# Differential attention's queries and keys: two token-major products of 256 columns made into one of 512

## The chip, the core and the metric

The kernel runs on one core of a Trainium2 chip. The metric is the device time of one execution in microseconds (us); lower is better. The time before is the median of three runs, and one more execution was profiled.

## What is computed

Two layers of a hybrid trunk run over 384 tokens of width 1024: 128 context tokens and 256 latent tokens, which share all weights. A layer normalises its input, then runs three token mixers in parallel (a convolution module, differential attention, latent attention), merges them with gates, and ends in an MLP. The part that matters here is the projection of the normalised input `h` to the queries, keys and values of differential attention: three matrices of 1024 by 512, four heads of 2 times 64 columns each. Queries and keys are normalised over each 64 columns, and for the latent tokens rotated:

```python
proj = h @ P['w_in'][l]
u_conv, dq, dk, dv, cq, ckv, kpe, gl = jnp.split(proj, _split_points(), axis=-1)
q = _rms(dq.reshape(b, s, DIFF_HEADS, 2, DIFF_HD), P['diff_q_norm'][l])
k = _rms(dk.reshape(b, s, DIFF_HEADS, 2, DIFF_HD), P['diff_k_norm'][l])
v = dv.reshape(b, s, DIFF_HEADS, 2 * DIFF_HD)
...
q = _rope2d(q, tabs[0])
k = _rope2d(k, tabs[0])
```

The normalised keys and the values of the context tokens are outputs too.

## The kernel before

**Weights.** All weights lie in DRAM as pieces (`weight_pieces`, L69) of at most 1024 elements per partition, in the order in which they are used. A piece is loaded by SP (`raw`, L179), then split (`split`, L191) into a high part by ScalarE (L197) and a remainder by VectorE (L198). Four buffers hold high parts, three hold remainders. Every product takes three matmuls per block of 128 rows of the contraction (`passes`, L204 to L206): high by high, high by remainder, remainder by high.

**Two forms of product.** In the feature-major form (`fm`) the weights are stationary in the array and 384 token columns stream through. In the token-major form (`tm`, L229) a block of 128 tokens of `h` is stationary and columns of the weights stream through, 256 at a time for queries, keys and values. The projection has 8 blocks of contraction, 3 blocks of tokens and 3 passes, so one token-major product is 72 matmuls, whatever its columns. Each block of tokens accumulates in a PSUM bank of its own; the three `mm` banks are shared by all such products.

**The part that is changed.** `qkv(l, h, c)` (L594) runs twice per layer, once for each pair of heads c. It makes three products in a row: queries, keys, values (with 32 more columns for c = 1). After the products of queries and keys, ScalarE copies each bank to a tile `tok` (L619) and squares it (L591), VectorE sums the squares (L592), takes the reciprocal root in ten short operations (L309 to L319) and rotates (L581 to L585); the keys are scaled first (L634, L636). Then a flag `q0`, `k0`, `v0` and so on is raised.

**What orders the work.** Three generators are woven together (`weave`, L253): the dense products, the chain of transposes (`chains`), and the two attentions. A dense step tells how much of a unit it is worth (a unit is three passes of 384 columns, so three passes of 256 columns are 2/3). A side generator waits for a flag, then for a number of units from the table `W` (L134), then issues its next step. `qkv_T` (L642) waits for `q0`, then 12.5 units, and transposes the queries (L658); it then waits for `k0`, then 20 units, and transposes the keys. Attention c starts on the flags `kT` and `v` of that c. Where the dense generator itself waits for a flag, `weave` issues side steps without regard to their units until the flag is up. Such a place is `mla_kv` (L884): before the second half of its products it yields `mqT0` or `mqT1` (L893), which `mla_T` raises; for the second group of heads `mla_T` first waits for `m0` (L924), which the latent attention raises after its first pair of heads. After the weave a scheduler orders the instructions of each engine: it goes by priority, which follows the order of issue, and takes later work where the earlier isn't ready. So the convolution's long row of VectorE operations (L1071), which is issued late, fills VectorE's free time much earlier.

Of the kernel before, what the change touches and what calls it, by code (L numbers as in the profile page):

```python
# [17 lines left out]
ALU = mybir.AluOpType  # L18
# [3 lines left out]
P = 128  # L22
D = 1024
KD = 8
# [4 lines left out]
NT = 3  # L29
# [11 lines left out]
EPS = 1e-6  # L41
# [27 lines left out]
def weight_pieces():  # L69

    out = []

    def add(key, name, l, nkb, cols, per):
        for i, k0 in enumerate(range(0, nkb, per)):
            out.append(((l, *key, i), name, l, range(k0, min(k0 + per, nkb)), cols))

    def r(a, n):
        return list(range(a, a + n))

    def mod(l, s):  # L80
        for p in range(MODS[s][3]):
            a = MODS[s][0] * D + MODS[s][1] * p * P
            add(("mod", s, p), "mod_w", l, KD, r(a, P) + r(a + MODS[s][2] * P, P), 4)

    mod(0, 0)
    for l in range(L):
        for i in range(1 if l == 0 else AB):
            add(("u", i), "w_in", l, KD, r(512 + P * i, P) + r(P * i, P), 4)
        for c in range(2):
            for i in range(3):  # L90

                e = r(3200, 32) if (i, c) == (2, 1) else []
                add(("qkv", i, c), "w_in", l, KD, r(1024 + 512 * i + 256 * c, 256) + e, 3 if e else 4)
        add(("c", 0), "w_in", l, KD, r(2560, 256), 4)
        add(("c", 1), "w_in", l, KD, r(2816, 256), 4)
        add(("c", 2), "w_in", l, KD, r(3072, P), 8)
        for i in range(1 if l == 0 else AB, 4):
            add(("u", i), "w_in", l, KD, r(512 + P * i, P) + r(P * i, P), 4)
        for g in range(2):
            add(("uq", g), "w_uq", l, 3, r(384 * g, 384), 2)  # L100
            add(("ukv", g), "w_ukv", l, 2, r(512 * g, 512), 2)
            for i in range(4):
                add(("g", 1 + g, i), "w_in", l, KD, r(3232 + 1024 * (1 + g) + 256 * i, 256), 4)
            for i in range(4):
                n, w = (("od", "w_diff_out"), ("om", "w_mla_out"))[g]
                add((n, i), w, l, 4, r(256 * i, 256), 4)
        if l == 0:
            mod(0, 2)
            mod(0, 1)
        for i in range(4):  # L110
            add(("g", 0, i), "w_in", l, KD, r(3232 + 256 * i, 256), 4)
            add(("oc", i), "w_conv_out", l, 4, r(256 * i, 256), 4)
        for i in range(4):
            add(("wo", i), "w_out", l, KD, r(256 * i, 256), 4)
        for f in range(2):
            for i in range(8):
                add(("up", f, i), "w_up", l, KD, r(2048 * f + 256 * i, 256), 4)
            for i in range(4):
                for j, k0 in enumerate(range(16 * f, 16 * f + 16, 4)):
                    out.append(((l, "dn", f, i, j), "w_down", l, range(k0, k0 + 4), r(256 * i, 256)))  # L120
    return out


PIECES = weight_pieces()
WOFF = {}
_o = 0
# [20 lines left out]
class Body:  # L147
# [446 lines left out]
    def qkv(self, l, h, c):  # L594

        V, A, t = self.V, self.A, self.t
        d = self.d[c]
        v = self.tl(self.ap, [P, 4, 256], "v", 3)
        cs = slice(256 * c, 256 * c + 256)
        self.nc.gpsimd.dma_start(out=v[:, 3, :], in_=t["cv"][l][:, cs])  # L600
        d["v"] = v
        for i in range(3):
            if i < 2:
                xs = self.tl(self.ap, [P, NT, 256], "tok", 2)
                ss = self.tl(self.ap, [P, NT * 4], "ss", 2)
            pss = [self.psum("mm") for _ in range(NT)]
            e = (i, c) == (2, 1)
            yield from self.tm(pss, 288 if e else 256, [(l, "qkv", i, c, k) for k in range(3 if e else 2)],
                               [self.tok(h, tt) for tt in range(NT)])
            if e:  # L610
                self.pe = self.tl(self.ap, [P, 4, 32], "pe", 1)
                self.nc.sync.dma_start(out=self.pe[:, 3, :], in_=t["cpe"][l])
            for tt, ps in enumerate(pss):
                if i == 2:
                    A.copy(v[:, tt, :], ps[:, :256])
                    if e:
                        V.tensor_copy(self.pe[:, tt, :], ps[:, 256:288])
                    continue
                A.copy(xs[:, tt, :], ps[:, :256])  # L619
                self.sumsq(ss[:, 4 * tt : 4 * tt + 4], xs[:, tt, :].rearrange("p (n d) -> p n d", d=64), 0.125, 4, 64)  # L620
            if i == 2:
                self.nc.scalar.dma_start(out=t["nv"][l][:, cs], in_=v[:, 0, :])
                self.flags.add(f"v{c}")
                continue
            V.tensor_scalar(ss, ss, EPS, None, op0=ALU.add)
            y = self.rsqrt(ss, NT * 4)
            x4 = xs.rearrange("p t (n d) -> p t n d", d=64)
            if i == 0:
                d["qsc"] = self.tl(self.ap, [P, 32], "qsc", 3)[:, : NT * 4]
                V.tensor_scalar(d["qsc"], y, 0.125, None, op0=ALU.mult)  # L630
                self.rope(x4[:, 1:3], self.tab["dq"], 4, 64)
            else:
                xf = xs.rearrange("p t (n d) -> p (t n) d", d=64)
                V.tensor_tensor(xf, xf, y.unsqueeze(2).to_broadcast([P, NT * 4, 64]), ALU.mult)  # L634
                dk = self.rowt[:, ROW["dk"][0] : ROW["dk"][1]]
                V.tensor_tensor(x4[:, 0], x4[:, 0], dk.unsqueeze(1).to_broadcast([P, 4, 64]), ALU.mult)  # L636
                self.nc.scalar.dma_start(out=t["nk"][l][:, cs], in_=xs[:, 0, :])
                self.rope(x4[:, 1:3], self.tab["dk"], 4, 64)
            d["qk"[i]] = xs
            self.flags.add(f"{'qk'[i]}{c}")  # L640

    def qkv_T(self, l, c):  # L642

        A, E = self.A, self.E
        d = self.d[c]
        for i in range(2):
            yield f"{'qk'[i]}{c}"
            yield W["qT"] if i == 0 else W["kT"]
            if i == 0:
                dst = d["qT"] = self.tl(self.ap, [P, 2, T], "qT", 3)  # L650
            else:
                dst = d["kT"] = self.tl(self.ap, [P, 2, NK], "kT", 3)
                self.nc.gpsimd.dma_start(out=dst[:, :, T:], in_=self.t["ckT"][l][:, 2 * c : 2 * c + 2, :])
            xs = d["qk"[i]]
            for hh in range(2):
                pt = self.psum("tr")
                for j in range(NT):
                    E.transpose(pt[:, j * P : j * P + P], xs[:, j, hh * P : hh * P + P], self.ident)  # L658
                if i == 0:
                    a, b = PV["dq"]  # L660
                    A.activation(dst[:, hh, 0:P], pt[:, 0:P], AF.Identity, scale=self.pv[l][:, a:b])
                    A.copy(dst[:, hh, P:T], pt[:, P:T])
                else:
                    A.copy(dst[:, hh, 0:T], pt[:, :T])
        self.flags.add(f"kT{c}")
# [827 lines left out]
```

## Time and profile before

| what | us |
|---|---|
| median of three runs | 1348.26 |
| lowest and highest run | 1346.23, 1349.81 |
| the profiled execution | 1349.73 |
| its span in the trace | 1347.9 |
| TensorE busy | 1325.7 (98%) |
| TensorE weight loads | 1252.0 (93%) |
| VectorE busy | 1058.2 (79%) |
| ScalarE busy | 681.3 (51%) |

The profiled execution lies 1.47 us above the median, and its span 1.83 us below its own time. A busy TensorE isn't a TensorE at its peak: a matmul's recorded duration includes its latency and overlaps the next, so its cost in a stream is read from the distance between two starts.

### The profile page before, as it was taken

The numbers are of one execution on the slowest core, as the hardware profiler recorded it, in microseconds if no ns is written. First come the engines' busy times: TensorE is split into PE (matmuls) and PEld (weight loads), VectorE is DVE, ScalarE is ACT, GpSimd is POOL, SyncE is SP. The second block draws the span as 40 slices with busy tenths as digits, with TensorE's granted clock in tenths as the row PEclk, the third lists the DMA queues.
The fourth block names the chain that finished last, engine by engine and source line by source line (L and its number), as shares of the span: only waits on it lengthen the run. The fifth ranks groups of instructions, "written<-read, shape, count | busy, mean of one in ns | idle before, by whom it ended". The sixth has DMA issues, their size and how long they took to land.

```text
span 1347.9 us, 21768 instructions
## 1 busy us (share of the span) xinstructions
PE 1325.7 (98%) x8096; PEld 1252.0 (93%) x8096; DVE 1058.2 (79%) x2517; ACT 681.3 (51%) x1281; POOL 16.7 (1%) x34
## 2 busy tenths in 40 slices
PE   5999999999999999999999999999999999999998
PEld 3999887879999999999999998888899999999998
DVE  5877999995998999974569779999999899333432
ACT  3555655454544762365335556665554467226621
POOL 0000000000000000000000000000000000000000
PEclk8999999999999999999999999999999999999999
DMA  9533334456574477764444333222347445333341
GB/s 361 187 96 113 123 127 148 156 175 216 162 254 131 145 245 248 253 203 126 149 149 141 99 97 114 69 95 94 125 163 244 157 157 188 125 126 126 127 148 54
DMA packets 62683, 209.46 MB, mean 155 GB/s; under 512 B 7840, under 2 KB 13600, under 8 KB 62320
## 3 DMA queue, kind: packets, MB, share of 16 engines
q1 hardware_dynamic: 56304, 196.93, 44.8%
q0 software_dynamic: 1808, 6.63, 1.5%
q10 hardware_dynamic: 4464, 4.50, 0.9%
q8 instruction: 64, 1.05, 0.3%
q14 instruction: 43, 0.35, 0.1%
HBM read 203.54 MB, written 4.49 MB: 154 GB/s over the span
## 4 chain that ended last, share of the span: by engine, by line
PE 93%; DVE 4%; DMA 1%; SPq 1%; ACT 0%; issue 0%; DVEq 0%
PE mm L204 19%; PE mm L206 19%; PE mm L205 19%; PE sc L204 9%; PE sc L205 9%; PE sc L206 9%; PE sc L759 3%; DMA wr<-wts 1%; PE av L996 1%; PE tr L981 1%; DVE wl L198 1%; PE mm L367 1%; PE av L821 1%; DVE z L1071 1%; PE tr L945 1%; PE tr L774 1%
## 5 line engine op out<-in xcount | busy, mean ns | idle before, releaser
L197 ACT CAST wh<-wr 128x1024 fp32r<-128x1024 f32 (+3 forms) x280 | 290.0, 1037 | 371.2 <-PE mm L205 189.5
L198 DVE TENSOR_TENSOR wl<-wr,wh 128x1024 fp32r<-128x1024 f32 (+3 forms) x280 | 336.7, 1203 | 132.6 <-PE mm L206 66.1
L204 PE MATMUL mm<-h,wh 128*128 128x384 f32 x848 | 291.2, 343 | 0.0
L206 PE MATMUL mm<-h,wl 128*128 128x384 f32 x848 | 286.3, 338 | 0.2 <-DVE wl L198 0.2
L205 PE MATMUL mm<-h,wh 128*128 128x384 f32 x592 | 200.1, 338 | 0.5 <-DVE h L440 0.5
L204 PEld LDWEIGHTS mm<-h,wh 128*128 128x128 f32 x848 | 159.8, 188 | 7.0 <-issue 2.9
L206 PEld LDWEIGHTS mm<-h,wl 128*128 128x128 f32 x848 | 159.5, 188 | 1.6 <-DVE wl L198 0.8
L1071 DVE SCALAR_TENSOR_TENSOR z<-u,dwh,z 128x399 f32<-128x399 f32 x240 | 147.2, 629 | 0.4
L395 DVE SCALAR_TENSOR_TENSOR ot<-wm,srow 128x1024 bf16<-128x1024 f32 x112 | 136.7, 1220 | 2.8 <-DMA wm<-modwT 2.2
L205 PEld LDWEIGHTS mm<-h,wh 128*128 128x128 f32 x592 | 111.6, 189 | 1.7 <-DVE h L440 0.8
L206 PE MATMUL sc<-h,wl 128*128 128x384 f32 x336 | 112.6, 335 | 0.0
L204 PE MATMUL sc<-h,wh 128*128 128x384 f32 x336 | 112.6, 335 | 0.0
L205 PE MATMUL mm<-o,wh 128*128 128x384 f32 x320 | 107.4, 336 | 0.0
L204 PE MATMUL mm<-x,wh 128*128 128x384 f32 (+1 forms) x288 | 97.3, 338 | 0.0
L206 PE MATMUL mm<-x,wl 128*128 128x384 f32 (+1 forms) x288 | 96.6, 336 | 0.0
L205 PE MATMUL mm<-x,wh 128*128 128x384 f32 (+1 forms) x288 | 96.6, 335 | 0.0
L204 PE MATMUL sc<-x,wh 128*128 128x384 f32 (+1 forms) x272 | 91.7, 337 | 0.0
L205 PE MATMUL sc<-x,wh 128*128 128x384 f32 (+1 forms) x272 | 91.2, 335 | 0.0
L206 PE MATMUL sc<-x,wl 128*128 128x384 f32 (+1 forms) x272 | 91.2, 335 | 0.0
L204 PE MATMUL mm<-wh,h 128*128 128x256 f32 (+1 forms) x288 | 83.1, 289 | 0.0
L206 PE MATMUL mm<-wh,h 128*128 128x256 f32 (+1 forms) x288 | 82.1, 286 | 0.0
L205 PE MATMUL mm<-wl,h 128*128 128x256 f32 (+1 forms) x288 | 82.0, 285 | 0.0
(275 smaller groups left out, 2564.7 us busy)
## 6 DMA issues: line engine op xcount, KB each, us to landing
wr<-wts SPq DMA_DIRECT2D x306, 512.0 KB, 3.5
wm<-modwT SPq DMA_DIRECT2D x56, 512.0 KB, 4.3
srow<-condrow POOLq DMA_DIRECT2D x2, 1024.0 KB, 7.7
wr<-wts SPq DMA_DIRECT2D x4, 432.0 KB, 3.4
G<-xT SPq DMA_DIRECT2D x8, 192.0 KB, 4.1
wr<-wts SPq DMA_DIRECT2D x4, 384.0 KB, 3.1
G<-xT POOLq DMA_DIRECT2D x8, 192.0 KB, 3.4
xd<-G ACTq DMA_DIRECT2D x8, 192.0 KB, 2.5
```

The costliest lines, as they stand in the source:

```text
L197: self.A.copy(hi[:, :n], w[:, :n])
L198: self.V.tensor_tensor(lo[:, :n], w[:, :n], hi[:, :n].bitcast(F32), ALU.subtract)
L204: self.E.matmul(ps, ah, bh, start=start, stop=False)
L205: self.E.matmul(ps, ah, bl, start=False, stop=False)
L206: self.E.matmul(ps, al, bh, start=False, stop=stop)
L367: E.matmul(ps[32 * j : 32 * j + 32, :256], self.cond[:, 4 * h + j, :], w[:, j * 256 : j * 256 + 256], start=h == 0, stop=h == 1, tile_posi ...
L395: V.scalar_tensor_tensor(j, w, 0.5, self.srow[:, c, :], ALU.mult, ALU.mult, accum_out=self.modT[l][:, b, c : c + 1])
L759: E.matmul(sc[:, :n], q[c][:, qs], k[c][:, ks], start=True, stop=True)
L774: self.E.transpose(pt[:, j : j + P], e[:, j : j + P], self.ident)
L821: E.matmul(av[:, hd * P : hd * P + P], wT[:, j * P : j * P + P], v[:, k0 // P + j, hd * P : hd * P + P], start=j == 0, stop=j == n // P - 1)
L945: E.transpose(pt[0:96, tt * P : tt * P + P], m["ks"][tt // 2][:, tt % 2, hh, :], self.ident)
L1071: self.V.scalar_tensor_tensor(z[b], self.u[:, b, k : k + ZW], self.dw[:, b * CK + k : b * CK + k + 1], z[b], ALU.mult, ALU.add)
```

## The change

The weights of queries and keys of one pair of heads are laid out as one piece of 512 columns (256 of the queries, 256 of the keys) with 2 blocks of contraction per piece, where before each had 256 columns and 4 blocks; the bytes and the number of pieces stay the same. `qkv` makes one product of 512 columns for both. Each PSUM bank is then filled to its 512 values and copied out in two halves, all six copies first; then come the squares, the roots and the rotation, queries first, keys after, and both flags are raised behind that one product. The product of the values follows as before.

```diff
-            for i in range(3):
-                e = r(3200, 32) if (i, c) == (2, 1) else []
-                add(("qkv", i, c), "w_in", l, KD, r(1024 + 512 * i + 256 * c, 256) + e, 3 if e else 4)
+            add(("qk", c), "w_in", l, KD, r(1024 + 256 * c, 256) + r(1536 + 256 * c, 256), 2)
+            e = r(3200, 32) if c == 1 else []
+            add(("v", c), "w_in", l, KD, r(2048 + 256 * c, 256) + e, 3 if e else 4)
...
-        for i in range(3):
-            if i < 2:
-                xs = self.tl(self.ap, [P, NT, 256], "tok", 2)
-                ss = self.tl(self.ap, [P, NT * 4], "ss", 2)
-            pss = [self.psum("mm") for _ in range(NT)]
-            e = (i, c) == (2, 1)
-            yield from self.tm(pss, 288 if e else 256, [(l, "qkv", i, c, k) for k in range(3 if e else 2)],
-                               [self.tok(h, tt) for tt in range(NT)])
...
-                A.copy(xs[:, tt, :], ps[:, :256])
-                self.sumsq(ss[:, 4 * tt : 4 * tt + 4], xs[:, tt, :].rearrange("p (n d) -> p n d", d=64), 0.125, 4, 64)
...
+        pss = [self.psum("mm") for _ in range(NT)]
+        yield from self.tm(pss, 512, [(l, "qk", c, k) for k in range(4)], [self.tok(h, tt) for tt in range(NT)])
+        for i in range(2):
+            d["qk"[i]] = self.tl(self.ap, [P, NT, 256], "tok", 2)
+        ss = [self.tl(self.ap, [P, NT * 4], "ss", 2) for _ in range(2)]
+        for tt, ps in enumerate(pss):
+            for i in range(2):
+                A.copy(d["qk"[i]][:, tt, :], ps[:, 256 * i : 256 * i + 256])
+        for i in range(2):
+            xs = d["qk"[i]]
+            for tt in range(NT):
+                self.sumsq(ss[i][:, 4 * tt : 4 * tt + 4], xs[:, tt, :].rearrange("p (n d) -> p n d", d=64), 0.125, 4, 64)
+            V.tensor_scalar(ss[i], ss[i], EPS, None, op0=ALU.add)
+            y = self.rsqrt(ss[i], NT * 4)
...
             self.flags.add(f"{'qk'[i]}{c}")
+        e = c == 1
+        pss = [self.psum("mm") for _ in range(NT)]
+        yield from self.tm(pss, 288 if e else 256, [(l, "v", c, k) for k in range(3 if e else 2)],
+                           [self.tok(h, tt) for tt in range(NT)])
...
+        for tt, ps in enumerate(pss):
+            A.copy(v[:, tt, :], ps[:, :256])
...
+        self.flags.add(f"v{c}")
```

## Rows read from the trace of the kernel before

**Rows 1.** The page: busy time of the engines, granted TensorE clock, chain that ended last.

```profile
PE 1325.7 (98%) x8096; PEld 1252.0 (93%) x8096; DVE 1058.2 (79%) x2517; ACT 681.3 (51%) x1281; POOL 16.7 (1%) x34
...
PEclk8999999999999999999999999999999999999999
...
PE 93%; DVE 4%; DMA 1%; SPq 1%; ACT 0%; issue 0%; DVEq 0%
```

**Rows 2.** TensorE's waits over the span: us in total, times, longest.

```profile
PE tr L327 <- DVE z L349: 10.8, 1, 10.8
PE av L367 <- DMA wr<-wts: 2.4, 2, 1.8
PE tr L774 <- DVE e L812: 2.1, 3, 0.9
```

**Rows 3.** Groups of instructions by shape, TensorE: busy us, mean ns | idle before.

```profile
L204 PE MATMUL mm<-wh,h 128*128 128x256 f32 x240 | 68.6, 286 | 0.0
L204 PE MATMUL mm<-wh,cq 128*128 128x512 f32 x24 | 9.8, 410 | 0.0
```

**Rows 4.** Timeline of TensorE in the queries' product: start us, us, instruction.

```profile
51.08 0.28 PE L204 MATMUL mm<-wh,h 128*128 128x256 f32 x1
...
66.07 0.28 PE L206 MATMUL mm<-wh,h 128*128 128x256 f32 x1
```

**Rows 5.** Timeline of TensorE in a row of products of 512 columns (layer 0).

```profile
250.99 0.39 PE L204 MATMUL mm<-wh,cq 128*128 128x512 f32 x1
...
253.30 0.39 PE L205 MATMUL mm<-wl,cq 128*128 128x512 f32 x1
...
255.12 0.39 PE L204 MATMUL mm<-wh,cch 128*128 128x512 f32 x1
...
256.29 0.39 PE L206 MATMUL mm<-wh,ccl 128*128 128x512 f32 x1
```

**Rows 6.** Busy time by stretch: length, PE, PEld, DVE, ACT, POOL, PEclk, DMA share, GB/s.

```profile
51.00:66.00 15.00, 15.00 (x127) 15.00 (x126) 12.87 (x48) 7.59 (x15) 0.00 (x0) 1.00 0.43 141
...
251.00:256.20 5.20, 5.20 (x24) 4.26 (x24) 5.03 (x13) 2.81 (x9) 0.00 (x0) 1.00 0.31 101
```

**Rows 7.** Groups of instructions by shape, ScalarE.

```profile
L197 ACT CAST wh<-wr 128x1024 fp32r<-128x1024 f32 x266 | 279.7, 1052 | 359.7 <-PE mm L205 184.6 <-PE sc L205 122.2 <-issue 23.1
...
L591 ACT ACTIVATE tmp<-tok 128x256 f32<-128x256 f32 x40 | 17.0, 425 | 0.7
L619 ACT COPY tok<-mm 128x256 f32<-128x256 f32 x24 | 9.0, 376 | 5.5 <-PE mm L206 5.4
```

**Rows 8.** Timeline of VectorE (last rotations) and TensorE (transposes), layer 0, c = 0.

```profile
63.24 0.43 DVE L585 TENSOR_TENSOR tok<-tok,tmp 128x256 f32<-128x256 f32 x1
...
66.19 0.82 PE L658 MATMUL tr<-ident,tok 128*128 128x128 f32 x6
79.79 0.82 PE L658 MATMUL tr<-ident,tok 128*128 128x128 f32 x6
```

**Rows 9.** Timeline of TensorE around the second half of `mla_kv`, layer 1.

```profile
906.83 0.82 PE L930 MATMUL tr<-ident,tok 128*96 128x128 f32 x6
...
911.65 0.39 PE L204 MATMUL mm<-wh,cq 128*128 128x512 f32 x1
```

**Rows 10.** Busy time by stretch in layer 1, columns as in rows 6.

```profile
747.00:772.00 25.00, 25.00 (x206) 23.74 (x205) 18.22 (x58) 13.96 (x37) 0.00 (x0) 1.00 0.36 104
...
860.00:930.00 70.00, 70.00 (x413) 62.34 (x412) 68.84 (x196) 41.73 (x92) 0.00 (x0) 1.00 0.30 98
```

**Rows 11.** Groups of instructions by shape, VectorE, in differential attention.

```profile
L760 DVE TENSOR_REDUCE nm<-sc 128x1 f32<-128x384 f32 x64 | 34.6, 552 | 1.8 <-PE sc L759 1.1
...
L812 DVE SCALAR_TENSOR_TENSOR e<-e,ra,e 128x384 f32<-128x384 f32 x16 | 9.8, 614 | 0.1
```

**Rows 12.** Timeline of TensorE where the convolution's output is used, layer 1.

```profile
984.40 0.80 PE L327 MATMUL tr<-ones,z 128*128 128x1 f32 x6
...
1004.07 0.34 PE L204 MATMUL mm<-h,wh 128*128 128x384 f32 x1
1004.25 0.54 PE L204 MATMUL sc<-cq,wh 128*128 128x384 f32 x2
```

**Rows 13.** Page, issues of the weight loads: KB each, us to landing.

```profile
wr<-wts SPq DMA_DIRECT2D x306, 512.0 KB, 3.5
```

More of the change, by code (lines that the diff above doesn't have):

```diff
@@ L601, in qkv @@
         d["v"] = v
-        for i in range(3):
-            if i < 2:
-                xs = self.tl(self.ap, [P, NT, 256], "tok", 2)
-                ss = self.tl(self.ap, [P, NT * 4], "ss", 2)
-            pss = [self.psum("mm") for _ in range(NT)]
-            e = (i, c) == (2, 1)
-            yield from self.tm(pss, 288 if e else 256, [(l, "qkv", i, c, k) for k in range(3 if e else 2)],
-                               [self.tok(h, tt) for tt in range(NT)])
[L610 to L618, printed above, removed]
-                A.copy(xs[:, tt, :], ps[:, :256])
-                self.sumsq(ss[:, 4 * tt : 4 * tt + 4], xs[:, tt, :].rearrange("p (n d) -> p n d", d=64), 0.125, 4, 64)
[L621 to L626, printed above, removed]
+        pss = [self.psum("mm") for _ in range(NT)]
[12 more added lines that the diff above has]
+            y = self.rsqrt(ss[i], NT * 4)
             x4 = xs.rearrange("p t (n d) -> p t n d", d=64)
@@ L638, in qkv @@
                 self.rope(x4[:, 1:3], self.tab["dk"], 4, 64)
-            d["qk"[i]] = xs
             self.flags.add(f"{'qk'[i]}{c}")
+        e = c == 1
+        pss = [self.psum("mm") for _ in range(NT)]
+        yield from self.tm(pss, 288 if e else 256, [(l, "v", c, k) for k in range(3 if e else 2)],
+                           [self.tok(h, tt) for tt in range(NT)])
+        if e:
+            self.pe = self.tl(self.ap, [P, 4, 32], "pe", 1)
+            self.nc.sync.dma_start(out=self.pe[:, 3, :], in_=t["cpe"][l])
+        for tt, ps in enumerate(pss):
+            A.copy(v[:, tt, :], ps[:, :256])
+            if e:
+                V.tensor_copy(self.pe[:, tt, :], ps[:, 256:288])
+        self.nc.scalar.dma_start(out=t["nv"][l][:, cs], in_=v[:, 0, :])
+        self.flags.add(f"v{c}")
     def qkv_T(self, l, c):
```

## Prediction

> **What bounds the kernel now.** I read the page first: engines, clock, chain [rows 1]. TensorE is busy 98% of the span, at the granted clock of full speed (2.4 GHz) in all slices but the first, and it carries 93% of the chain that ended last. A busy share can hide waiting, so the next view is TensorE's own waits [rows 2]: the one long wait, 10.8 us, lies at the start; the next largest are 2.4 and 2.1 us in total. So every stretch after the start is set by how densely matmuls follow one another. What a matmul costs is then not its recorded duration (286 ns for 256 columns, 410 ns for 512 [rows 3], with the latency in it) but the distance between starts. In the queries' product 126 matmuls of 256 columns start between 51.08 and 66.07 [rows 4]: 14.99 us over 125 steps, 0.1199 us each. The kernel already has products of 512 columns in token-major form, those of `mla_kv`: 24 of them start from 250.99 to 256.29 [rows 5], 5.30 us over 23 steps, 0.2304 us each. Both stretches have the clock at 1.00, so they can be compared [rows 6]. Weight loads overlap the stream in both: in the stretch of 256 columns their records fill all 15.00 us, in that of 512 only 4.26 of 5.20 [rows 6].
>
> **The product of queries and keys.** Before: 2 products of 72 matmuls, 2 pairs of heads, 2 layers, 576 matmuls of 256 columns by 0.1199 = 69.1 us. After: 288 of 512 columns by 0.2304 = 66.4 us. Saved: **2.7 us**, all on the path, for nothing else ends later than TensorE there. This is small, because the same columns still stream: two of 256 take 0.2398 us, one of 512 0.2304. The only thing that falls away is the second matmul's share beyond its columns. How much that is isn't certain. The 8 steps from 253.30 to 255.12 [rows 5] take 0.2275 each, which gives 288 x 0.0123 = 3.5 us; the last 5, from 255.12 to 256.29, take 0.2340, which gives 288 x 0.0058 = 1.7 us. I take the middle, since it is the mean of the whole row, and keep 1.7 to 3.5.
>
> The Trainium skill ("TensorE: Matmul & The Clock Gate", Back-to-back issue gap) gives an isolated gap of columns divided by 2.4 plus 2.5 ns. By it two matmuls of 256 would take 218.3 ns and one of 512 215.8, and the change would save 288 x 2.5 ns = 0.7 us. The trace doesn't agree: 119.9 and 230.4 ns, 13 to 17 ns over the columns' own time.
>
> **Weights.** Bytes, pieces (4 per pair of products) and columns per piece (1024 elements) stay. A piece lasts 36 x 0.12 = 4.3 us before and 18 x 0.23 = 4.1 us after. Its load lands in 3.5 us [rows 13], with four high buffers ahead, and its cast takes 1.05 us [rows 7]. ScalarE's casts wait mostly for TensorE to give a buffer back [rows 7], so the supply is ahead. Cost: 0; if that cover went, each piece could show at most its split.
>
> **Copies out of PSUM.** A bank is now read twice, 2 x 0.38 us [rows 7]. The last piece gives the three banks up one after another, 6 matmuls or 1.4 us apart; the first bank is done 2.8 us before the product ends, and the values' product, which wants it next, begins only then. Even with a cast in front (1.05 + 0.75) that is hidden. The next two banks have the same 2.8 us. Cost: 0, upper end 1 us in all.
>
> **The later flags.** Here something does move. The queries' flag now comes after one product of 32 units instead of after 16; the keys' flag stays at 32. Counted in units: queries were transposed 12.5 after 16, keys 20 after 32, at 52; now queries at 44.5 and keys at 64.5. Everything behind the transposed keys, that is, both differential attentions, starts 12.5 units later. Three passes of 256 columns are 2/3 of a unit and take 3 x 0.12 us, so a unit is 0.54 us, and 12.5 are **6.8 us**. (In the trace the transposes stand at 66.19 and 79.79 [rows 8]; I expect the first near 74 and the second near 86.) The queries' chain on VectorE ended 2.5 to 3 us before its transposes [rows 8]; now three more copies stand before its squares, 1.1 us, so it still fits. The keys' chain has 20 units more after that.
>
> What is late next? In layer 0 dense work waits for nothing: the second half of its second `mla_kv` comes some 26 units, 14 us, after the chain has raised what it needs. In layer 1 the margin is thin. The transposes that release that half are at 906.83, the half itself begins at 911.65 [rows 9]: 4.8 us, less than 6.8. So there the dense generator will block, and about two steps of the latent attention are issued at once instead of 8.6 units apart. The scheduler can put the branch products that follow into the gap, as it does for the convolution: a matmul of the next gate starts at 1004.07, ahead of the rest of the product that waits for `cq` [rows 12]. I cost the block at 0; its upper end, with nothing put in, is two steps of 8.6 x 0.54 = 9.3 us.
>
> Second, VectorE. It is free a quarter of the time early in layer 1 (18.22 of 25 us) and full later (68.84 of 70) [rows 10]. A unit of differential attention needs at least 2 x 0.552 + 0.614 = 1.7 us of it [rows 11], every 10 units of weave; 12.5 units later means some 2.2 us of work moved from the free part into the full one, and the convolution, which fills the rest, ends so much later. Its sum of squares is picked up at 984.40, its result wanted by 1004 [rows 12]. What covers 2.2 us is the next gate's product, 48 matmuls. Cost 0, upper end 2.2 us; below nothing neither can go, for no work is taken away.
>
> **Sum.** -2.7 us. Against the profiled execution 1349.73 - 2.7 = 1347.0; that execution lies 1.47 us above the median, so the median goes from 1348.26 to **1345.6 us**. That is 0.2%: less than the 0.3% (4.0 us) which a measurement of this kernel can tell from no change.
>
> **Rivals.**
> *Faster by more.* The best spacing holds throughout (3.5 us), and the shifted attention lets the waits of the transposes on `e` (2.1 us [rows 2]) go. Together 5.6 us: 1342.7. For it: nothing else uses PSUM or SBUF heavily in the keys' product. Against: those waits move with the attention rather than vanish.
>
> *Slower.* The block in layer 1 decides. If the scheduler cannot fill it, because the banks or weight buffers that the branch products want are taken, TensorE stands still for up to 9.3 us: 1345.6 + 9.3 = 1354.9. It makes the kernel slower from 2.7 us of standing, measurably so from 6.7. For it: VectorE is full just there, so each forced step is slow. Against: TensorE's waits are tiny everywhere, though VectorE is full for 70 us on end [rows 2, 10]; the scheduler has filled such gaps before.
>
> *No saving.* The spacing of 512 columns in a long stream is that of the worst stretch or worse: 1.7 us or less, 1347.0 by the rows. For it: a stream of 72 has never run here. The skill's gap above would end there too, at 1347.5.
>
> **How the numbers follow.** Forecast (about -2.7, within 0.3%): 0.50. No saving: 0.12, also within. Faster by more: 0.20. Slower: 0.18, of which two thirds (0.12) pass 0.3% and the rest (0.06) stays within. This gives faster 0.20, same 0.68, slower 0.12. The range: below, 3.5 us of saving and some stalls gone, 1341.5; above, half of the slower rival's standing and the upper ends of copies and VectorE, 1345.6 + 6 = 1351.5. What is left out is the full block, some 0.1, and a larger gain, under 0.1.
>
> **What would show it.** Right: 288 matmuls `mm<-wh,h` of 512 columns, 0.2275 to 0.234 us from start to start; 72 of them in 16.6 us; transposes of layer 0 near 74 and 86 us; the values' product starting without a gap; TensorE's waits as small as now; in layer 1 branch products drawn ahead of the second half of `mla_kv`. Wrong: a gap of TensorE of several us near 910 or 1004, matmuls of 512 columns closer than 0.22 us, or a new wait for a PSUM bank between queries-and-keys and values.

## The result: 17 us slower, and the profile after

The changed kernel took **1365.72 us** (median of four runs, 1364.04 to 1366.55) beside 1348.35 (four runs, 1346.23 to 1349.81) for the kernel before: a ratio of 1.0126, 95% interval 1.0113 to 1.0139, 17.4 us. That is slower, and far outside the range of the prediction. The profiled execution took 1364.04 us.

The page of the changed kernel, as in [rows 1]:

```profile
span 1362.3 us, 21195 instructions
...
PE 1331.0 (98%) x7808; PEld 1241.5 (91%) x7808; DVE 1054.9 (77%) x2517; ACT 679.9 (50%) x1281; POOL 16.7 (1%) x34
...
PEclk9998999999999999999999989999999999999999
```

TensorE has 288 matmuls fewer and is still 98% busy; by the page alone nothing has happened. But the clock has two new dips, the 8s in the fourth and the twenty-fourth slice, one in each layer. TensorE's waits (line waited for: us in total, times, longest) say what happened there:

```profile
PE tr L327 <- DVE z L349: 11.0, 1, 11.0
PE tr L776 <- DVE nm L764: 8.8, 2, 4.4
...
PE mm L204 <- ACT v L907: 1.2, 1, 1.2
```

The second row is new: two waits of 4.4 us, where the transposes of the same tile `e` had waited 0.9 us at most [rows 2]. The next view is TensorE's timeline of the changed kernel, layer 0 (start us, us, instruction, idle before it with the releaser):

```profile
47.83 0.39 PE L205 MATMUL mm<-wl,h 128*128 128x512 f32 x1
...
63.74 0.39 PE L206 MATMUL mm<-wh,h 128*128 128x512 f32 x1
63.97 0.28 PE L204 MATMUL mm<-wh,h 128*128 128x256 f32 x1
...
105.39 0.29 PE L206 MATMUL mm<-wh,h 128*128 128x288 f32 x1
110.10 0.87 PE L776 MATMUL tr<-ident,e 128*128 128x128 f32 x3 [4.42 <-DVE nm L764]
110.62 0.67 PE L204 MATMUL mm<-h,wh 128*128 128x384 f32 x1
...
115.89 0.37 PE L205 MATMUL mm<-h,wh 128*128 128x384 f32 x1
...
120.92 0.33 PE L204 MATMUL mm<-h,wh 128*128 128x384 f32 x1
...
122.83 0.34 PE L206 MATMUL mm<-h,wl 128*128 128x384 f32 x1
...
790.82 0.87 PE L776 MATMUL tr<-ident,e 128*128 128x128 f32 x3 [4.42 <-DVE nm L764]
```

Three things stand here. First, the new product itself: 71 matmuls of 512 columns start from 47.83 to 63.74, 70 steps of 0.2273 us, and the values' product follows at once. Second, the stand: the last matmul of the values' product of the second pair (288 columns) starts at 105.39, and nothing follows until the transposes of `e` at 110.10. `e` belongs to the differential attention of the *first* pair. Third, what comes after the stand: the matmuls of 384 columns from 110.62 to 115.89 take 16 steps of 0.329 us, those from 120.92 to 122.83 take 11 of 0.174, and the latter is the rate of a clock at 1.00.

What VectorE did while TensorE stood is in its timeline, changed kernel, same columns:

```profile
103.95 0.95 DVE L624 TENSOR_TENSOR tok<-tok,nwy 128x768 f32<-128x768 f32 x1
104.82 0.15 DVE L812 RECIPROCAL ra<-s 128x1 f32<-128x1 f32 x1
...
105.58 1.23 DVE L198 TENSOR_TENSOR wl<-wr,wh 128x1024 fp32r<-128x1024 f32 x1 [0.16 <-PE mm L205]
106.73 0.42 DVE L626 TENSOR_TENSOR tok<-tok,row 128x256 f32<-128x256 f32 x1
107.06 0.69 DVE L581 TENSOR_TENSOR tmp<-tok,sgdk 128x128 f32<-128x128 f32 x3
...
108.88 0.21 DVE L813 SCALAR_TENSOR_TENSOR ra<-ra,s,neglam 128x1 f32<-128x1 f32 x1
109.00 0.41 DVE L585 TENSOR_TENSOR tok<-tok,tmp 128x256 f32<-128x256 f32 x1
109.34 0.61 DVE L814 SCALAR_TENSOR_TENSOR e<-e,ra,e 128x384 f32<-128x384 f32 x1
109.87 0.15 DVE L764 TENSOR_TENSOR nm<-nm,qsc 128x2 f32<-128x2 f32 x1
```

L812, L813 and L814 are three steps in a row of one softmax: take the reciprocal of the sum, scale it, combine the two maps to `e`. By themselves they take 0.15 + 0.21 + 0.61 us. Here 4.52 us pass from the start of L812 to the start of L814, and in between stand a remainder of weights (L198) and the scaling and rotation of the second pair's keys (L626, L581 to L585), whose transposes start only at 123.01 us. VectorE ran the long operations first and the short steps L813 and L814 at the end of them. L764, the scaled maximum of the next softmax, came after them too. The waits name `nm` L764 as the releaser, since it came last before 110.10; the tile that TensorE transposes there is `e`, and its writer, L814, ends at 109.95.

In the kernel before, the same chain stood between the same two steps, and did little harm. The lines of TensorE and VectorE there, layer 0, for the softmax that met it:

```profile
99.02 0.92 PE L759 MATMUL sc<-kT,qT 64*128 64x384 f32 x4
99.96 1.02 DVE L760 TENSOR_REDUCE nm<-sc 128x1 f32<-128x384 f32 x2 [0.27 <-PE sc L759]
...
103.08 0.15 DVE L810 RECIPROCAL ra<-s 128x1 f32<-128x1 f32 x1
...
103.84 0.95 DVE L634 TENSOR_TENSOR tok<-tok,nwy 128x768 f32<-128x768 f32 x1
...
107.99 0.61 DVE L812 SCALAR_TENSOR_TENSOR e<-e,ra,e 128x384 f32<-128x384 f32 x1
...
108.75 0.52 PE L774 MATMUL tr<-ident,e 128*128 128x128 f32 x3 [0.91 <-DVE e L812]
```

From the reciprocal to `e` it was 4.91 us, longer than in the changed kernel, and the transposes waited 0.91 us. What the changed kernel adds lies ahead of the reciprocal. Its lines for the softmax of the 4.42 us wait:

```profile
94.98 0.92 PE L761 MATMUL sc<-kT,qT 64*128 64x384 f32 x4
...
99.36 0.55 DVE L762 TENSOR_REDUCE nm<-sc 128x1 f32<-128x384 f32 x1
```

The first maximum starts 4.38 us after its scores, where it was 0.94 before; until then VectorE works at the second pair's queries (rotation and roots), at the sums of the keys' squares and at a remainder of weights. So one softmax meets both chains: from its scores to `e` it takes 14.36 us, against 8.97 in the kernel before. TensorE had work for 10.7 us of that (94.98 to 105.68), and in the kernel before for 8.8 (99.02 to 107.84). From the start of L814 or L812 to the transposes it is 0.76 us in both kernels. What the softmax takes with that beyond TensorE's own work is the wait: 4.4 us, and 0.9 before. Layer 1 repeats it: scores at 775.70, first maximum at 780.08, `e` at 790.07.

The busy time by stretch of the changed kernel (length, PE, PEld, DVE, ACT, POOL, PEclk, DMA share, GB/s) shows both halves of the price:

```profile
106.00:110.20 4.20, 0.10 (x1) 0.14 (x2) 4.20 (x14) 1.18 (x3) 0.00 (x0) 0.87 0.52 166
110.20:117.50 7.30, 7.30 (x29) 7.05 (x29) 1.91 (x11) 1.78 (x6) 0.00 (x0) 0.61 0.03 6
```

While TensorE stands, VectorE is busy 4.20 of 4.20 us. Afterwards TensorE's granted clock is 0.61 in the mean. It stands "busy" 7.30 of 7.30 us, at half its rate for most of them, which is why the page's 98% says nothing.

### The profile page after: what moved, and what is told of

Read it like the earlier page. It is cut to its first block, busy times and chain, and to the rows that moved or that the text cites. A ratio compares the mean times of both kernels' runs of the same rounds, so it can differ in the third digit from the quotient of the medians.

```text
span 1362.3 us, 21195 instructions
## 1 busy us (share of the span) xinstructions
PE 1331.0 (98%) x7808; PEld 1241.5 (91%) x7808; DVE 1054.9 (77%) x2517; ACT 679.9 (50%) x1281; POOL 16.7 (1%) x34
## 4 chain that ended last, share of the span: by engine, by line
PE 93%; DVE 4%; DMA 1%; ACT 1%; issue 0%; SPq 0%; DVEq 0%; ACTq 0%
PE mm L204 19%; PE mm L205 19%; PE mm L206 19%; PE sc L204 9%; PE sc L205 9%; PE sc L206 9%; PE sc L761 3%; PE av L998 1%; PE mm L367 1%; DVE wl L198 1%; DMA wr<-wts 1%; PE tr L983 1%; DVE z L1073 1%; PE av L823 1%; PE tr L776 1%; ACT wh L197 1%
## 5 line engine op out<-in xcount | busy, mean ns | idle before, releaser
L198 DVE TENSOR_TENSOR wl<-wr,wh 128x1024 fp32r<-128x1024 f32 (+3 forms) x280 | 336.2, 1202 | 154.5 <-PE mm L206 73.3
L768 ACT ACTIVATE e<-sc,nm,qsc 128x384 f32<-128x384 f32 (+1 forms) x96 | 57.2, 602 | 19.3 <-DVE nm L764 18.7
L204 PE MATMUL mm<-wh,h 128*128 128x512 f32 (+2 forms) x192 | 66.2, 345 | 0.0
L205 PE MATMUL mm<-wl,h 128*128 128x512 f32 (+2 forms) x192 | 65.3, 340 | 0.0
```

The source lines that it names most:

```text
L198: self.V.tensor_tensor(lo[:, :n], w[:, :n], hi[:, :n].bitcast(F32), ALU.subtract)
L204: self.E.matmul(ps, ah, bh, start=start, stop=False)
L205: self.E.matmul(ps, ah, bl, start=False, stop=False)
L768: A.activation(e[:, :n], parts[c], AF.Exp, bias=nm[:, c : c + 1], scale=scale[:, c : c + 1], accum_out=s1[:, c : c + 1])
```

## The experiments

The expectations name three theories. **A, collision:** the scaling and rotation of the second pair's keys fall between two steps of the first pair's softmax on VectorE. (By the lines above such a meeting was there before too and cost 0.91 us; what A needs is that the moved chains hold one softmax for longer than TensorE has work.) **B, lateness:** everything behind the transposed keys comes 12.5 units later, wherever VectorE's queue stands. **C, width:** the product of 512 columns is itself the cost. Unless something else is said, an edit is made to the changed kernel. The kernel before, run again beside them, took 1348.1 to 1348.5 us.

**The keys' chain behind the values' product.** The product of 512 columns and the six copies stay; squares, roots, rotation and flag of the keys are issued only after the product of the values.

```diff
-        for i in range(2):
+        def chain(i):
...
+        chain(0)
         e = c == 1
...
         self.flags.add(f"v{c}")
+        chain(1)
```

> One product of 512 columns as in the change, but the squares, roots and rotation of the keys and the flag of the keys are issued behind the values' product. Theory A (in the changed kernel the keys' chain of VectorE stands in its queue between two steps of a softmax of the first differential attention, so that TensorE's transpose of e waits 4.4 us per layer and then runs some 7 us at the half clock; 7 us per layer): in this order the keys' chain falls behind the softmax's maximum, under its exponentials, and holds up only its last step: a wait of 1 to 2.5 us per layer, 1350 to 1357 us. Theory B (everything behind the keys' transposes starts 12.5 units later and the blocks behind it cost the time): the transposes of the keys come 3.5 units later still, so as slow as the change or slower, 1365 to 1369. Theory C (matmuls of 512 columns with their full banks cost more than the trace showed): 1365.

Measured: 1348.78 us (ten runs, 1348.25 to 1352.48), ratio 1.0010, interval 1.0001 to 1.0019. The 17 us are gone, though the keys are now transposed later still, at 68 units instead of 64.5. B alone can't explain that, and C can't either, since the wide product is in it. VectorE's timeline of this kernel, for the softmax that answers to the one above:

```profile
102.76 0.15 DVE L815 RECIPROCAL ra<-s 128x1 f32<-128x1 f32 x1
...
103.21 0.62 DVE L817 SCALAR_TENSOR_TENSOR e<-e,ra,e 128x384 f32<-128x384 f32 x1
...
106.75 0.15 DVE L767 TENSOR_TENSOR nm<-nm,qsc 128x2 f32<-128x2 f32 x1
106.83 0.95 DVE L624 TENSOR_TENSOR tok<-tok,nwy 128x768 f32<-128x768 f32 x1
```

From the reciprocal to `e` it is 0.45 us, and the long scaling (L624) starts only when the steps of this softmax, and the maxima of the next, are through. From the scores (97.30) to `e` it takes 5.9 us.

**The transposes early again.** The units before the transposes are cut to 8 and 12, so that the keys' stand at 52 as in the kernel before. (Of the table `W` only the two entries are shown, here and below.)

```diff
-"qT": 12.5, "kT": 20,
+"qT": 8, "kT": 12,
```

> The change with the table of units at 8 for the queries' transposes and 12 for the keys', so that the keys' transposes and the first attention stand at 52 units again, where they stood before the change; the chains of VectorE are issued as in the change. Theory A: what counts is where the keys' chain falls among the softmax steps; here its ten short steps lie between two softmaxes and its rotation under an exponential, so at most a short wait, 1346 to 1352 us. Theory B: the lateness is gone for the first pair of heads and with it the loss: 1345 to 1348. Theory C: 1365.

Measured: 1356.61 us (four runs), ratio 1.0063 (1.0047 to 1.0079). None of the theories gave this. The 4.4 us waits are gone, but new ones are scattered about; which of them make up the 8.2 us was not settled. TensorE's waits in this kernel:

```profile
PE tr L947 <- DVE tok L914: 1.8, 2, 1.5
...
PE tr L660 <- DVE tok L585: 1.3, 4, 0.5
```

The second row is the transposes that were pulled forward; four times they now wait for their rotation, 1.3 us in all.

**Two narrow products, both chains behind the second.** Weights, products and piece sizes of the kernel before; only the order of the change.

```diff
...
+            pss = [self.psum("mm") for _ in range(NT)]
+            yield from self.tm(pss, 256, [(l, "qk", i, c, k) for k in range(2)], [self.tok(h, tt) for tt in range(NT)])
             d["qk"[i]] = self.tl(self.ap, [P, NT, 256], "tok", 2)
+            for tt, ps in enumerate(pss):
+                A.copy(d["qk"[i]][:, tt, :], ps[:, :256])
...
```

> Two products of 256 columns as in the kernel before, each copied out at once, but both chains of VectorE and both flags are issued behind the second product, as in the change. Theory A: the keys' chain stands between the maximum and its scaling again, so a wait of some 4 us per layer with the half clock behind it, as in the change; without the 2.7 us that the wider matmuls save, 1364 to 1370 us. Theory B: the flags come as late as in the change, the same 1364 to 1370. Theory C: the matmuls are the old ones, 1347 to 1350.

Measured: 1357.11 us (four runs), ratio 1.0066 (1.0050 to 1.0083): slower without any wide product, so C falls. But A and B both expected the full loss here, and it didn't come. VectorE's timeline of this kernel:

```profile
99.67 0.55 DVE L762 TENSOR_REDUCE nm<-sc 128x1 f32<-128x384 f32 x1
100.14 0.95 DVE L624 TENSOR_TENSOR tok<-tok,nwy 128x768 f32<-128x768 f32 x1
...
104.29 0.15 DVE L764 TENSOR_TENSOR nm<-nm,qsc 128x2 f32<-128x2 f32 x1
104.41 0.43 DVE L586 TENSOR_TENSOR tok<-tok,tmp 128x256 f32<-128x256 f32 x1
...
106.87 0.16 DVE L812 RECIPROCAL ra<-s 128x1 f32<-128x1 f32 x1
...
107.32 0.62 DVE L814 SCALAR_TENSOR_TENSOR e<-e,ra,e 128x384 f32<-128x384 f32 x1
```

The keys' chain does stand between two steps of the softmax, as expected: between the maximum (99.67) and its scaling (104.29), 4.6 us. But this is the only long hold. From the scores (98.00) to `e` the softmax takes 9.3 us, not 14.36, and its transposes at 108.36 wait for nothing. So a chain between two steps is no loss by itself. Why the chains ran earlier there than in the change wasn't settled. The 8.7 us that are lost have no single large wait: the longest that [rows 2] doesn't have are 1.3, 1.2 and 0.9 us.

**The softmax first.** The direct test of A: the products, flags and units of the change, only the maxima, the scaled maximum and the three steps to `e` get priority with the scheduler, so that the chains are less likely to be put between them.

```diff
-                V.tensor_reduce(nm[:, c : c + 1], sc[:, :n], AX.X, ALU.max, negate=True)
+                with self.tc.high_priority(AHEAD):
+                    V.tensor_reduce(nm[:, c : c + 1], sc[:, :n], AX.X, ALU.max, negate=True)
...
+            with self.tc.high_priority(AHEAD):
+                V.reciprocal(ra, s1[:, hd, 1:2])
+                V.scalar_tensor_tensor(ra, ra, s1[:, hd, 0:1], self.neglam, ALU.mult, ALU.mult)
+                V.scalar_tensor_tensor(es[0][:, :n], es[1][:, :n], ra, es[0][:, :n], ALU.mult, ALU.add)
```

> The change with one thing more: maxima, their scaling and the combination of the two softmaxes get a higher priority in the scheduler, so that on VectorE they go ahead of the keys' chain; flags and units are those of the change. Theory A: the two waits of 4.4 us and the half clock behind them go, 14 of the 17 us: 1346 to 1354 us. Theory B: nothing starts earlier, 1362 to 1367. Theory C: 1365.

Measured: 1351.47 us (nine runs, 1349.89 to 1352.96), ratio 1.0023 (1.0014 to 1.0033): 14.25 us less than the change. VectorE's timeline of this kernel, then its busy time by stretch:

```profile
100.47 0.15 DVE L815 RECIPROCAL ra<-s 128x1 f32<-128x1 f32 x1
...
101.22 0.61 DVE L817 SCALAR_TENSOR_TENSOR e<-e,ra,e 128x384 f32<-128x384 f32 x1
...
107.81 0.16 DVE L815 RECIPROCAL ra<-s 128x1 f32<-128x1 f32 x1
...
108.54 0.61 DVE L817 SCALAR_TENSOR_TENSOR e<-e,ra,e 128x384 f32<-128x384 f32 x1
```

```profile
100.00:125.00 25.00, 23.95 (x151) 21.26 (x150) 20.94 (x68) 16.82 (x39) 0.00 (x0) 1.00 0.36 116
775.00:800.00 25.00, 23.97 (x151) 21.28 (x150) 20.98 (x68) 16.95 (x39) 0.00 (x0) 1.00 0.34 98
```

The same two stretches of the changed kernel:

```profile
100.00:125.00 25.00, 20.58 (x108) 18.17 (x107) 16.18 (x52) 13.35 (x31) 0.00 (x0) 0.86 0.29 94
775.00:800.00 25.00, 20.58 (x117) 17.50 (x117) 19.77 (x71) 11.82 (x28) 0.00 (x0) 0.86 0.29 93
```

The first two lines are the softmax that took 14.36 us in the change: from its scores (95.32) to `e` it takes 5.9 us here. The last two are the next softmax, beside the keys' chain: 0.73 us from reciprocal to `e`. The clock is at 1.00 in both layers as in the kernel before (24.09 us of TensorE busy, clock 1.00, in each of these stretches), and 151 matmul records stand where the change has 108 and 117. That is A. The priority covers the maxima as well as the steps to `e`, so this run doesn't tell the two holds apart.

**The priority alone, in the kernel before.** The hunk above, put on the kernel before:

```diff
+                with self.tc.high_priority(AHEAD):
...
+        with self.tc.high_priority(AHEAD):
...
+            with self.tc.high_priority(AHEAD):
```

> The kernel before (products of 256 columns, chains spread) with the higher priority of the softmax steps alone: what that priority is worth without the change. In the profile of the kernel before the same transposes wait 2.1 us in all for the combined weights. Theory A (the priority takes away a collision that the change made): it can give no more than those 2 us, 1346 to 1350. If the priority by itself were worth some 14 us, the run with it on the changed kernel would say nothing of the change: 1335.

Measured: 1352.74 us (seven runs), ratio 1.0033 (1.0021 to 1.0044). The priority gains nothing of its own; it costs 4.3 us there. So the 14.25 us above are not the priority's own; they are the collision's, less whatever the priority cost in that kernel.

**Lateness alone, in the kernel before.** Only the keys' transposes, and with them both attentions, come 12.5 units later.

```diff
-"kT": 20,
+"kT": 32.5,
```

> The kernel before, with the keys' transposes 32.5 units behind their flag instead of 20: everything behind them starts as late as in the change (64.5 units), while products and chains of VectorE are the old ones. This prices the lateness by itself. Theory A: there is no long wait of the transposes of e, and lateness is a matter of scattered small waits: 1349 to 1355. Theory B: the lateness is the loss: 1363 to 1368.

Measured: 1353.55 us (five runs, 1352.22 to 1356.78), ratio 1.0041 (1.0026 to 1.0057), 5.1 us. So moving these transposes costs something too, about a third of the loss. That this is lateness as such isn't shown: the priority of the experiment before, which moves no flag and no transpose, cost 4.3 us in the same kernel. And the attention came later here than in the change: counted from the first dense matmul, the first transposes of `e` came 5.5 us later than in the kernel before, in the change 3.45. TensorE's waits in this kernel:

```profile
PE mm L204 <- ACT tok L870: 1.9, 1, 1.9
PE tr L774 <- DVE e L812: 1.7, 4, 0.7
```

The first is the only large one that [rows 2] doesn't have; the rest is spread.

**Five more kernels,** none of them faster than the one before. First the kernel of the first experiment with its keys' transposes pulled forward:

```diff
-"kT": 20,
+"kT": 12.5,
```

> As the kernel with the keys' chain behind the values' product, but with 12.5 units instead of 20 before the keys' transposes, which then stand at 60.5 units (52 in the kernel before, 64.5 in the change, 68 in that kernel). Theory A: no collision, the lateness mostly taken back: 1344 to 1349 us, perhaps faster than before. Theory B: lateness of 8.5 units costs two thirds of 17 us: 1357 to 1360.

Measured: 1352.68 us (nine runs), ratio 1.0033 (1.0023 to 1.0043), a miss: the transposes of `e` now wait 2.2 us in all, in three places. Then the same kernel of the first experiment with the softmax first:

```diff
+        chain(1)
...
+            with self.tc.high_priority(AHEAD):
```

> The keys' chain behind the values' product and the higher priority of the softmax steps together. Theory A: both take away the same collision, so they don't add: 1345 to 1351. If the two acted on different losses, their gains (17 and 14 us) would add as far as there is loss left, and it would come near the 1345.7 that the wider matmuls alone allow.

Measured: 1349.53 us (ten runs), ratio 1.0010 (1.0001 to 1.0019), as without the priority. Both edits remove the same loss, so they don't add up. Then the first experiment's order with narrow products, which shows what the width is worth with the order held:

```diff
-        yield from self.tm(pss, 512, [(l, "qk", c, k) for k in range(4)], [self.tok(h, tt) for tt in range(NT)])
...
+            yield from self.tm(pss, 256, [(l, "qk", i, c, k) for k in range(2)], [self.tok(h, tt) for tt in range(NT)])
...
+        chain(1)
```

> Two products of 256 columns, the queries' chain behind the second, the keys' chain behind the values' product: the order of the kernel that ran 1348.8 us with the product of 512 columns. This prices the width of the matmuls with the order held. If 512 columns save 2.7 us, this takes about 2.7 us more: 1350 to 1353. Theory C (wide matmuls cost): it is faster than 1348.

Measured: 1354.0 us (five runs), ratio 1.0042 (1.0029 to 1.0055). The wide product is 5.2 us faster at this order, more than its spacing explains (3.6 us, below); the rest wasn't taken apart. The time is 1 us above the range expected. Then the change with its keys transposed at 52 units, the queries left at 44.5, without and with the softmax first:

```diff
-"kT": 20,
+"kT": 7.5,
```

> The change with 7.5 units instead of 20 before the keys' transposes: they stand at 52 units as in the kernel before, the queries' at 44.5 as in the change; the chains are issued as in the change. Theory A: the keys' rotation falls behind a finished softmax here, with two casts among it, before the next maxima, and can hold those up by 1 to 2 us; the lateness of 5 us is taken back: 1346 to 1352. Theory B: lateness gone: 1345 to 1347.

```diff
-"kT": 20,
+"kT": 7.5,
...
+            with self.tc.high_priority(AHEAD):
```

> The same with the higher priority of the softmax steps. Theory A: with collision and lateness both gone only the saving of the wide matmuls and the 4 us that this priority cost the kernel before are left: 1346 to 1351.

Measured: 1354.82 us (four runs), ratio 1.0054 (1.0038 to 1.0069), and 1359.47 us (four runs), ratio 1.0088 (1.0074 to 1.0102). Both miss. With the keys' transposes back at 52 units the change still loses 6.7 us, though its transposes of `e` no longer wait 4.4 us, and with the priority it loses more. TensorE's waits in the second one point to a reason:

```profile
PE tr L660 <- DVE tok L585: 4.7, 4, 2.1
PE tr L660 <- DVE ra L815: 2.0, 2, 1.0
```

It looks like the collision the other way round: the softmax now passes the rotation, and the transposes of queries and keys wait for that, 6.7 us in all. No run tests this.

**The kernel before, profiled once more,** unedited.

> The kernel before once more, for a second profile: the first profile came 1.4 us over the median and its products started 1.4 us later than those of the other profiles. If that is the start of that one execution, this profile has its first dense matmul near 23 us; if it belongs to the kernel, near 24.4.

Measured: 1348.64 us. Its first dense matmul, from TensorE's timeline:

```profile
23.25 0.54 PE L204 MATMUL mm<-h,wh 128*128 128x384 f32 x1 [0.51 <-ACT wh L197]
```

In the first profile of the same kernel it started at 24.39 us, in that of the change at 22.99. The start thus varies from one execution to another by a microsecond and more, and a difference of two spans carries that.

## Why the prediction was wrong

**Width: right in kind, a little too small.** I took 2.7 us, with 3.5 as the best end. In the changed kernel 512 columns take 0.2273 us, so 288 x (0.2398 - 0.2273) = **3.6 us** are saved. The best of the spacings in [rows 5], 0.2275, was the right one, and the mean of that whole row was not. One reading was loose and did no harm: the 126 matmuls of 256 columns are more than the 72 of the queries' product and run into the keys', at the same spacing. The isolated gap of the Trainium skill ("TensorE: Matmul & The Clock Gate", Back-to-back issue gap) works out at 215.8 ns for 512 columns at full clock; the trace, with 227.3, still disagrees.

**Weights and copies: right.** No wait for a PSUM bank stands behind the new product: the values' product starts at 63.97, 0.23 us behind the last matmul.

**The later flags: the step that failed.** It said "The queries' chain on VectorE ended 2.5 to 3 us before its transposes [rows 8]; now three more copies stand before its squares, 1.1 us, so it still fits. The keys' chain has 20 units more after that." Both held: the queries' and the keys' transposes of the first pair came 4.6 and 2.3 us later (70.80 and 82.11 us; 6.0 and 3.7 with the earlier start of 1.40), less than I expected, and no chain was late for its own transposes. But I asked only whether a chain is in time for the one who waits for *it*, not who is queued behind it on VectorE, and put the moved work of VectorE at 0, 2.2 us at most. In the kernel before the queries' and the keys' chain followed a product each, one product apart, and the softmax that met the keys' chain had its maxima at once. With the change they start together behind one product, and in the second pair they lie in the 18 units of the values' product; there one softmax of the first pair met both, 14.36 us from scores to `e` instead of 8.97. The price in each layer is read off above. The stand is 4.42 us. The clock behind it costs (5.27 - 16 x 0.174) = 2.5 us in layer 0 and, by the same reckoning over 11 steps from 791.35 to 795.01, 1.75 us in layer 1. From the transposes to the matmul behind them it is 0.52 us, where the kernel with two narrow products has 0.25 (108.36 to 108.61): 0.27 in each layer. Together 2 x 4.42 + 2.5 + 1.75 + 0.5 = **13.6 us**. In the kernel before a wait of 0.91 us stood in each layer, so 11.8 of this are new. The softmax with priority gave back 14.25, the keys' chain behind the values' product 16.9.

**"Counted at 0": lateness.** I costed the block in layer 1 at nothing, with an upper end of 9.3 us. Moving the keys' transposes alone costs **5.1 us** in the kernel before, and not as one block. The place that I named, `mla_kv` in layer 1, shows one small wait, in the changed kernel's waits the 1.2 us for `v` L907.

The sum is -3.6 + 11.8 + 5.1 = 13.3 us. The two profiled executions differ by 14.4 us in span and by 15.8 counted from the first dense matmul; the medians by 17.4. So 1 to 4 us are assigned to nothing, and the 5.1 us were measured in the kernel before, at a larger delay, and are only assumed for the changed one. The sum doesn't carry over to other orders: with the keys' transposes at 52 units neither of its two costs is left, and that kernel is still 6.7 us slower than the one before instead of 3.6 faster. What it loses stays open.

**The rivals.** "Slower" had the right sign and, with 1354.9, 11 us too little; its mechanism (TensorE standing, because dense work is blocked by a flag) and its place near 910 us were wrong. TensorE stood for the softmax, near 105 and 786 us. It got 0.18, because I took small waits over the whole span as a sign that the scheduler fills any gap. They may as well have been a sign of how well the units in `W` fitted the old flags. Every kernel here that moved a flag, a chain or a priority, the first experiment and its variant with priority aside, lost 3 to 11 us against the one before. "Faster by more" asked for the best spacing, which came, and for waits on `e` that go, and those grew. "No saving" is out by the spacing; its 1347.0 was also wrong in itself, since 1348.26 - 1.7 is 1346.6. And the upper end of the range left out part of what it names: half of 9.3, 1 and 2.2 are 7.9 us, not 6, which gives 1353.5. The measured time lies beyond that too.

## What to carry to other kernels

When a change moves a chain of small operations, ask not only whether the chain is still in time, but between which steps of other work it will stand on its engine's queue: read that engine's timeline at the new place, add up how long all the moved chains together hold one critical chain, and set that beside the work that the waiting engine has left meanwhile: here one hold of 4.9 us cost 0.9 us, and two on the same softmax cost a stand of 4.4. A hand-tuned order with few waits was fragile here rather than robust: to price a move, first try the same move alone in the old kernel, as was done here with the keys' transposes. And a stand of TensorE is to be priced with the slow matmuls behind it: 4.4 us were 6.4 to 7.2 here.

## What the runs showed of the chip

The stand cost more than its length, and I had not counted that. After 4.4 us without work TensorE's granted clock read 0.61 in the mean of the next 7.3 us: matmuls of 384 columns started 0.32 us apart until 115.89, the 1.2 GHz level, and 0.174 us apart afterwards, at 2.4 GHz. The second stand, as long as the first, was followed by 11 slow steps instead of 16. The Trainium skill ("TensorE: Matmul & The Clock Gate", HAM oscillation — how this bites in real kernels) describes such a fall of the clock after a wait for data; the trace agrees, with a wait for another engine's queue in the DMA's place.
